# A row softmax: from tile-managed waits and two DMA queues to own semaphores, one queue in a fixed order, and loops on ScalarE

## The chip, the cores and the metric

The kernel runs on one core of a Trainium2 chip. The metric is the device time of one execution in microseconds; lower is better. A core has five engines with instruction streams of their own that meet only through semaphores: TensorE (PE, not used here), VectorE (DVE), ScalarE (ACT), GpSimd (POOL) and SyncE (SP). Beside them 16 DMA engines move data between the chip's memory and the core's on-chip memory. SP and ACT can each issue transfers, each into a DMA queue of its own; both queues are served by the same 16 DMA engines.

## The reference

```python
def setup_inputs():
    batch, seq, dim = 16, 1024, 512
    return {"x": np.random.randn(batch, seq, dim).astype(np.float32)}

def reference(x):
    x_max = np.max(x, axis=-1, keepdims=True)
    exp_x = np.exp(x - x_max)
    return (exp_x / np.sum(exp_x, axis=-1, keepdims=True)).astype(np.float32)
```

It is a softmax over 16,384 rows of 512 float32 values. All of the input, 33.55 MB, is read once and as much is written once.

## The kernel before

The rows are cut into 8 chunks of 2,048 rows. In a chunk each of the 128 partitions holds 16 rows of 512 values, 32 KB, so that a chunk is one transfer of 4,096 KB. On chip there are 6 places (`held`); chunk k lies in place k mod 6, is computed in place, and is stored from there. Chunks 6 and 7 therefore go into the places of chunks 0 and 1, once these have been stored. A chunk is handled in two groups of 8 rows a partition, so there are 16 groups, g = 0 to 15; chunk k is groups 2k and 2k + 1.

The work on one group:

- `rowmax` (line 89): DVE takes the negated maximum of each of the 8 rows in one reduction over 128 x 4,096 elements, into `shift`.
- `exps` (line 94): ACT computes exp(x + shift) row by row, 8 instructions of 128 x 512, each leaving its row's sum in `sums`. The 128 such instructions stand one after the other in ACT's program.
- `scale` (lines 105 to 114): DVE takes the reciprocal of the 8 sums. For groups 0 to 12 POOL multiplies the whole group with it in one instruction of 128 x 4,096 (line 107); for groups 13 to 15 DVE does it row by row, 8 instructions of 128 x 512 (line 114).

The order on each engine is that of the text, written out by hand: for each g the maximum of g, the exponentials of g, then the scaling of g - 1. The waits between the engines are put in by the tile layer, which owns the buffers and their semaphores.

Transfers: SP issues the loads (line 72), ACT the stores (line 75). Loads 0 to 5 are issued at the start, the very first ahead of the barrier at which all engines meet at the kernel's start (`loads_at_the_head`). Loads 6 and 7 stand in SP's program behind stores 0 and 1 and wait for them. A store stands in ACT's program between exponentials, up to two groups later than the last scaling of its chunk (`STORE_BEHIND`). Loads lie in DMA queue q1, stores in q10.

Behind the last store comes the closing work of the tile layer (line 161): SP waits for the outstanding transfers, then all engines meet twice, and the semaphores are cleared between.

Of the kernel before, what the change touches and what calls it, by code (L numbers as in the profile page):

```python
# [1 line left out]

# [4 lines left out]

F32 = mybir.dt.float32
EXP = mybir.ActivationFunctionType.Exp
AX = mybir.AxisListType.X  # L10


CHUNK = 16
CHUNKS = 8
PLACES = 6
GROUP = 8

STORE_BEHIND = [1, 1, 1, 1, 0, 0, 0, 0]

LOAD_AFTER = {0: 6, 1: 7}  # L20
ON_POOL = 13


AT_HEAD = {mybir.EngineType.SP: 1}

def loads_at_the_head(nc):

    main, body = nc.main_func.blocks[0], nc.main_func.blocks[1]  # L30
    for engine, count in AT_HEAD.items():
        loads = [
            i
            for i in body.instructions
            if i.engine == engine and type(i).__name__ == "InstDMACopy"
        ][:count]
        barrier = next(
            n
            for n, i in enumerate(main.instructions)
            if i.engine == engine and type(i).__name__ == "InstDrain"  # L40
        )
        for load in loads:
            body.instructions.remove(load)
        main.instructions[barrier:barrier] = loads


@with_exitstack
def kernel(
    ctx: ExitStack,
    tc: tile.TileContext,  # L50
    x: bass.AP,
    out: bass.AP,
):
    nc = tc.nc
    nc.at_finalize(loads_at_the_head)
    P = nc.NUM_PARTITIONS

    x_rows = x.flatten_outer_dims().rearrange("(c p r) d -> c p r d", p=P, r=CHUNK)
    out_rows = out.flatten_outer_dims().rearrange("(c p r) d -> c p r d", p=P, r=CHUNK)
    n, _, _, d = x_rows.shape  # L60
    assert n == CHUNKS

    data = ctx.enter_context(tc.tile_pool(name="data", bufs=1))
    stats = ctx.enter_context(tc.tile_pool(name="stats", bufs=6))
    held = data.tile([P, PLACES * CHUNK, d], F32, name="held")

    def place(k):
        at = (k % PLACES) * CHUNK
        return held[:, at : at + CHUNK, :]

    def load(k):
        nc.sync.dma_start(out=place(k), in_=x_rows[k])  # L72

    def store(k):
        nc.scalar.dma_start(out=out_rows[k], in_=place(k))
        if k in LOAD_AFTER:
            load(LOAD_AFTER[k])

    per = CHUNK // GROUP
    groups = CHUNKS * per  # L80
    shift, sums = [None] * groups, [None] * groups

    def rows(g):
        at = (g % per) * GROUP
        return place(g // per)[:, at : at + GROUP, :]

    def rowmax(g):
        shift[g] = stats.tile([P, GROUP], F32, name="shift", tag="shift")
        nc.vector.reduce_max(out=shift[g], in_=rows(g), axis=AX, negate=True)  # L89

    def exps(g):
        sums[g] = stats.tile([P, GROUP], F32, name="sums", tag="sums")
        for r in range(GROUP):
            nc.scalar.activation(  # L94
                out=rows(g)[:, r, :],
                in_=rows(g)[:, r, :],
                func=EXP,
                bias=shift[g][:, r : r + 1],
                scale=1.0,
                accum_out=sums[g][:, r : r + 1],  # L100
            )

    def scale(g):
        recip = stats.tile([P, GROUP], F32, name="recip", tag="recip")
        nc.vector.reciprocal(out=recip, in_=sums[g])  # L105
        if g < ON_POOL:
            nc.gpsimd.tensor_mul(  # L107
                out=rows(g),
                in0=rows(g),
                in1=recip.unsqueeze(2).to_broadcast([P, GROUP, d]),  # L110
            )
            return
        for r in range(GROUP):
            nc.vector.tensor_scalar_mul(  # L114
                out=rows(g)[:, r, :],
                in0=rows(g)[:, r, :],
                scalar1=recip[:, r : r + 1],
            )

    with tc.manual_schedule():  # L120
        for k in range(PLACES):
            load(k)
        stored = 0
        for g in range(groups):
            rowmax(g)
            exps(g)
            if g:
                scale(g - 1)
            if stored < CHUNKS and g > (stored + 1) * per - 1 + STORE_BEHIND[stored]:
                store(stored)  # L130
                stored += 1
        scale(groups - 1)
        while stored < CHUNKS:
            store(stored)
            stored += 1


# [1 line left out]
_INS = ['x']  # L139
_OUTS = [((16, 1024, 512), 'float32')]  # L140


# [23 lines left out]
```

## Time and profile before

| what | value |
|---|---|
| device time, median of 3 runs | 161.96 us (161.58 to 162.31) |
| span of the profiled execution, first to last instruction | 160.4 us |
| that execution's own device time | not listed apart from the three runs |
| DVE / ACT / POOL busy | 82.0 / 92.7 / 91.0 us |
| memory read / written | 33.55 / 33.55 MB |
| mean rate over the span | 419 GB/s |

The page of the profile gives, for one execution, the busy time of each engine; the span in 40 slices, in which a digit is the busy share in tenths; the DMA queues; the chain of work that ended last; and groups of equal instructions with their mean duration and the idle time before them. A window view gives for any stretch the busy time of each engine, the granted clock of TensorE (1.00 throughout; TensorE isn't used), the mean busy share of the 16 DMA engines, and the rate in GB/s. A packet's whole time and bytes count where it starts, so in short windows the share can exceed 1.

### The profile page before, as it was taken

What the parts mean: (1) busy time and instruction counts of PE and PEld (TensorE: products, weight loads), DVE (VectorE), ACT (ScalarE), POOL (GpSimd) and SP (SyncE); (2) the same over time, 40 slices, a digit from 0 to 9 for tenths busy, and PEclk for the clock granted to TensorE, in tenths of its full rate; (3) what the DMA queues carried; (4) which work ended last, traced back from release to release, by engine and by line L of the source; (5) the groups of instructions that cost most, each with busy time, mean ns of one, the idle gap of its engine ahead of it and who ended that gap; (6) DMA issues with size and microseconds to landing.
All of it is one profiled execution on the core that took longest, in us unless ns stands there. A gap on an engine that the chain in (4) does not pass through costs nothing.

```text
span 160.4 us, 425 instructions
## 1 busy us (share of the span) xinstructions
DVE 82.0 (51%) x56; ACT 92.7 (58%) x257; POOL 91.0 (57%) x17
## 2 busy tenths in 40 slices
DVE  0009967977977700893009920099202999671000
ACT  0003899999998996079900959409594195920000
POOL 0000039999999999999993899508995000000000
DMA  7999999999899999999999999999999999999993
GB/s 261 482 433 392 466 449 392 443 458 400 343 433 400 449 449 409 425 474 409 425 466 409 409 490 409 402 466 441 400 449 449 409 425 474 411 409 474 425 392 139
DMA packets 2307, 67.13 MB, mean 419 GB/s; under 512 B 256, under 2 KB 256, under 8 KB 256
## 3 DMA queue, kind: packets, MB, share of 16 engines
q1 hardware_dynamic: 1152, 33.55, 49.5%
q10 hardware_dynamic: 1152, 33.55, 48.5%
q14 instruction: 3, 0.02, 0.0%
HBM read 33.55 MB, written 33.55 MB: 418 GB/s over the span
## 4 chain that ended last, share of the span: by engine, by line
DMA 53%; POOL 14%; DVE 10%; ACT 7%; issue 7%; DVEq 0%; SPq 0%
DMA held<-in_x_dram 34%; DMA out_dram<-held 19%; POOL held L107 14%; ACT held L94 7%; DVE shift L89 6%; DVE held L114 4%; DVE recip L105 0%; DVEq L161 0%; SPq L72 0%; DVEq L105 0%; DVEq L89 0%
## 5 line engine op out<-in xcount | busy, mean ns | idle before, releaser
L94 ACT ACTIVATE held<-held,shift 128x512 f32<-128x512 f32 x128 | 90.6, 719 | 36.4 <-DVE shift L89 32.0
L107 POOL TENSOR_TENSOR held<-held,recip 128x4096 f32<-128x4096 f32 x13 | 90.8, 7018 | 31.5 <-DVE recip L105 31.5
L89 DVE TENSOR_REDUCE shift<-held 128x8 f32<-128x4096 f32 x16 | 70.2, 4393 | 46.9 <-DMA held<-in_x_dram 46.9
L94 ACT ACTIVATION_READ_ACCUMULATOR held<-held,shift 128x1 f32 x128 | 25.3, 198 | 0.0
L105 DVE RECIPROCAL recip<-sums 128x8 f32<-128x8 f32 x16 | 3.2, 200 | 16.0 <-ACT held L94 16.0
L114 DVE TENSOR_SCALAR held<-held,recip 128x512 f32<-128x512 f32 x24 | 9.8, 483 | 0.1
L94 ACT ACT_TABLE_LOAD x1 | 1.3, 1283 | 12.3 <-DMA held<-in_x_dram 12.3
L150 POOL MEMSET const-float32-0.0<- 128x1 f32 x1 | 0.1, 99 | 0.2 <-issue 0.2
L150 POOL MEMSET const-bfloat16-1.0<- 128x1 bf16 x1 | 0.1, 102 | 0.0
L150 POOL MEMSET const-uint8-127<- 128x1 uint8 x1 | 0.1, 102 | 0.0
L150 POOL MEMSET const-float32-1.0<- 128x1 f32 x1 | 0.1, 99 | 0.0
## 6 DMA issues: line engine op xcount, KB each, us to landing
held<-in_x_dram SPq DMA_DIRECT2D x8, 4096.0 KB, 41.8
out_dram<-held ACTq DMA_DIRECT2D x8, 4096.0 KB, 28.0
```

What stands on the lines that cost most here:

```text
L89: nc.vector.reduce_max(out=shift[g], in_=rows(g), axis=AX, negate=True)
L94: nc.scalar.activation(out=rows(g)[:, r, :], in_=rows(g)[:, r, :], func=EXP, bias=shift[g][:, r : r + 1], scale=1.0, accum_out=sums[g][:, ...
L105: nc.vector.reciprocal(out=recip, in_=sums[g])
L107: nc.gpsimd.tensor_mul(out=rows(g), in0=rows(g), in1=recip.unsqueeze(2).to_broadcast([P, GROUP, d]),)
L114: nc.vector.tensor_scalar_mul(out=rows(g)[:, r, :], in0=rows(g)[:, r, :], scalar1=recip[:, r : r + 1],)
L150: nc = _bacc.Bacc("TRN2", target_bir_lowering=False, num_devices=1)
```

## The change

The kernel is written anew around the same chunks, places and groups, with these differences:

- The three statistics lie in memory of their own, one column for each group (128 columns each), and the buffers are allocated outside the tile layer.
- The tile layer is closed (`tc.close()`) right behind the issue of the six first loads. What it does at its end, the two meetings of all engines, then stands there in the program. Everything behind it waits on semaphores of the kernel's own: one for each load (`loaded`), each store (`stored`) and each chunk's scaling (`scaled`), and one each for maxima, exponentials and reciprocals. `take` waits until a semaphore has n and takes n off again.
- All transfers are issued by SP into one queue, in the order of `ORDER`: loads 0 to 5, stores 0 to 2, loads 6 and 7, stores 3 to 7. Ahead of each store SP waits for both groups of its chunk, ahead of loads 6 and 7 for stores 0 and 1. At the end SP waits for stores 2 to 7.
- ACT's exponentials become two loops at run time: 12 turns over groups 0 to 11 and 4 turns over groups 12 to 15, each turn with a wait, eight exponentials whose addresses come from registers, and a jump back. The table for exp is loaded ahead of the first wait.
- POOL scales groups 0 to 11 and DVE groups 12 to 15, both with one instruction of 128 x 4,096 a group (line 144 of the new kernel).
- DVE's order stays: the maximum of g, then the reciprocal and, from group 12, the product of g - 1.

```diff
-STORE_BEHIND = [1, 1, 1, 1, 0, 0, 0, 0]
-LOAD_AFTER = {0: 6, 1: 7}
-ON_POOL = 13
+ORDER = [("L", k) for k in range(PLACES)] + [
+    ("S", 0), ("S", 1), ("S", 2), ("L", 6), ("L", 7),
+    ("S", 3), ("S", 4), ("S", 5), ("S", 6), ("S", 7),
+]
+ON_VECTOR = (12, 13, 14, 15)
...
-    def load(k):
-        nc.sync.dma_start(out=place(k), in_=x_rows[k])
-
-    def store(k):
-        nc.scalar.dma_start(out=out_rows[k], in_=place(k))
-        if k in LOAD_AFTER:
-            load(LOAD_AFTER[k])
...
+    def take(engine, semaphore, n):
+        engine.wait_ge(semaphore, n).then_inc(semaphore, -n)
...
+    with tc.manual_schedule():
+        for _, k in ORDER[:PLACES]:
+            first = nc.sync.dma_start(out=place(k), in_=x_rows[k])
+            first.then_inc(loaded[k], 16)
+            tc.no_tile_sem_insts.add(first.ins.name)
+    tc.close()
+    tc.compile()
+
+    reused = set()
+    for what, k in ORDER[PLACES:]:
+        if what == "L":
+            if k >= PLACES:
+                take(nc.sync, stored[k - PLACES], 16)
+                reused.add(k - PLACES)
+            nc.sync.dma_start(out=place(k), in_=x_rows[k]).then_inc(loaded[k], 16)
+        else:
+            take(nc.sync, scaled[k], PER)
+            nc.sync.dma_start(out=out_rows[k], in_=place(k)).then_inc(stored[k], 16)
...
     def scale(g):
-        recip = stats.tile([P, GROUP], F32, name="recip", tag="recip")
-        nc.vector.reciprocal(out=recip, in_=sums[g])
-        if g < ON_POOL:
-            nc.gpsimd.tensor_mul(...)
-            return
-        for r in range(GROUP):
-            nc.vector.tensor_scalar_mul(...)
+        engine, ready = (
+            (nc.vector, to_vector) if g in ON_VECTOR else (nc.gpsimd, to_pool)
+        )
+        take(nc.vector, expd, 1)
+        nc.vector.reciprocal(out=stats(recip, g), in_=stats(sums, g)).then_inc(ready, 1)
+        take(engine, ready, 1)
+        engine.tensor_mul(
+            out=rows(g),
+            in0=rows(g),
+            in1=stats(recip, g).unsqueeze(2).to_broadcast([P, GROUP, d]),
+        ).then_inc(scaled[g // PER], 1)
...
+    nc.scalar.preload_act_table(EXP)
+
+    def exps(first, turns):
+        with nc.scalar.Fori(0, turns) as i:
+            take(nc.scalar, maxed, 1)
+            for r in range(GROUP):
+                row = held[:, bass.ds(i * GROUP + r, 1), :]
+                at = bass.ds(i * GROUP + (first * GROUP + r), 1)
+                act = nc.scalar.activation(
+                    out=row, in_=row, func=EXP,
+                    bias=shift[:, at], scale=1.0, accum_out=sums[:, at],
+                )
+            act.then_inc(expd, 1)
+
+    exps(0, RING)
+    exps(RING, GROUPS - RING)
+
+    for k in range(CHUNKS):
+        if k not in reused:
+            take(nc.sync, stored[k], 16)
```

More of the change, by code (lines that the diff above doesn't have):

```diff
@@ L61 @@
     assert n == CHUNKS
-    data = ctx.enter_context(tc.tile_pool(name="data", bufs=1))
-    stats = ctx.enter_context(tc.tile_pool(name="stats", bufs=6))
-    held = data.tile([P, PLACES * CHUNK, d], F32, name="held")
+    held = nc.alloc_sbuf_tensor("held", [P, PLACES * CHUNK, d], F32).ap()
+    shift = nc.alloc_sbuf_tensor("shift", [P, GROUPS * GROUP], F32).ap()
+    sums = nc.alloc_sbuf_tensor("sums", [P, GROUPS * GROUP], F32).ap()
+    recip = nc.alloc_sbuf_tensor("recip", [P, GROUPS * GROUP], F32).ap()
+    loaded = [nc.alloc_semaphore(f"loaded{k}") for k in range(CHUNKS)]
+    stored = [nc.alloc_semaphore(f"stored{k}") for k in range(CHUNKS)]
+    maxed = nc.alloc_semaphore("maxed")
+    expd = nc.alloc_semaphore("expd")
+    to_pool = nc.alloc_semaphore("to_pool")
+    to_vector = nc.alloc_semaphore("to_vector")
+    scaled = [nc.alloc_semaphore(f"scaled{k}") for k in range(CHUNKS)]
+    def take(engine, semaphore, n):
+        engine.wait_ge(semaphore, n).then_inc(semaphore, -n)
     def place(k):
@@ L69, in place @@
         return held[:, at : at + CHUNK, :]
-    def load(k):
-        nc.sync.dma_start(out=place(k), in_=x_rows[k])
-    def store(k):
-        nc.scalar.dma_start(out=out_rows[k], in_=place(k))
-        if k in LOAD_AFTER:
-            load(LOAD_AFTER[k])
-    per = CHUNK // GROUP
-    groups = CHUNKS * per
-    shift, sums = [None] * groups, [None] * groups
-    def rows(g):
-        at = (g % per) * GROUP
-        return place(g // per)[:, at : at + GROUP, :]
-    def rowmax(g):
-        shift[g] = stats.tile([P, GROUP], F32, name="shift", tag="shift")
-        nc.vector.reduce_max(out=shift[g], in_=rows(g), axis=AX, negate=True)
@@ L91, in exps @@
-    def exps(g):
-        sums[g] = stats.tile([P, GROUP], F32, name="sums", tag="sums")
-        for r in range(GROUP):
[L94 to L101, printed above, removed]
-    def scale(g):
-        recip = stats.tile([P, GROUP], F32, name="recip", tag="recip")
-        nc.vector.reciprocal(out=recip, in_=sums[g])
-        if g < ON_POOL:
[L107 to L111, printed above, removed]
-            return
[L113 to L135, printed above, removed]
+    def rows(g):
+        at = (g % RING) * GROUP
+        return held[:, at : at + GROUP, :]
@@ new lines, in stats @@
+    def stats(t, g):
+        return t[:, g * GROUP : (g + 1) * GROUP]
+    with tc.manual_schedule():
[15 more added lines that the diff above has]
+            nc.sync.dma_start(out=out_rows[k], in_=place(k)).then_inc(stored[k], 16)
@@ new lines, in rowmax @@
+    def rowmax(g):
+        if g % PER == 0:
+            take(nc.vector, loaded[g // PER], 16)
+        nc.vector.reduce_max(
+            out=stats(shift, g), in_=rows(g), axis=AX, negate=True
+        ).then_inc(maxed, 1)
+    def scale(g):
+        engine, ready = (
[9 more added lines that the diff above has]
+        ).then_inc(scaled[g // PER], 1)
@@ new lines @@
+    for g in range(GROUPS):
+        rowmax(g)
+        if g:
+            scale(g - 1)
+    scale(GROUPS - 1)
+    nc.scalar.preload_act_table(EXP)
[6 more added lines that the diff above has]
+                act = nc.scalar.activation(
+                    out=row,
+                    in_=row,
+                    func=EXP,
+                    bias=shift[:, at],
+                    scale=1.0,
+                    accum_out=sums[:, at],
+                )
+            act.then_inc(expd, 1)
```

13 lines of the change are left out of this document (added).

## The prediction

> **What bounds the kernel now.** I read the page from the top: busy shares, the 40 slices, the DMA queues, then the chain of waits, and last windows of the span.
>
> ```profile
> span 160.4 us, 425 instructions
> DVE 82.0 (51%) x56; ACT 92.7 (58%) x257; POOL 91.0 (57%) x17
> DMA  7999999999899999999999999999999999999993
> q1 hardware_dynamic: 1152, 33.55, 49.5%
> q10 hardware_dynamic: 1152, 33.55, 48.5%
> q14 instruction: 3, 0.02, 0.0%
> held<-in_x_dram SPq DMA_DIRECT2D x8, 4096.0 KB, 41.8
> ```
>
> No compute engine is busy for 60% of the span. The DMA line reads 9 nearly everywhere, and the two data queues (q1 loads, q10 stores) together hold 98.0% of the 16 DMA engines' span. So the sixteen transfers of 4096 KB (4.194 MB) set the time, and the question for any edit is whether it changes how fast the DMA engines run, when they start, or what follows them. Next, the rate in windows:
>
> ```profile
> core 0: us, DVE busy (x) ACT busy (x) POOL busy (x), PEclk, DMA share, GB/s
> 3.00:37.00 34.00, 20.89 (x8) 21.56 (x58) 14.20 (x3) 1.00 1.01 435
> 37.00:42.00 5.00, 3.84 (x3) 5.00 (x15) 5.00 (x1) 1.00 1.02 347
> 42.00:123.00 81.00, 38.33 (x18) 54.63 (x154) 71.60 (x11) 1.00 1.00 433
> 123.00:157.00 34.00, 18.95 (x29) 11.53 (x32) 0.00 (x0) 1.00 1.00 431
> ```
>
> The last column is what moved. Loads alone in one queue (3 to 37) run at 435 GB/s, loads and stores mixed from two queues (42 to 123) at 433, stores alone in one queue (123 to 157) at 431. One stretch stands out: at the first store (37 to 42) only 347 GB/s. What is missing there is (435 - 347) x 5 / 435 = 1.0 us of the DMA engines' time. Then the head and the tail, from the chain, the stores' landings, the wait list of SP's queue and two short windows:
>
> ```profile
> 0.00 12.25 DMA held<-in_x_dram
> ```
> ```profile
> L75 ACTq DMA_DIRECT2D out_dram<-held x8: 338/338/377, 36.8 to 145.0; - x8
> DMA to landing us min/median/max: 14.5/28.0/41.5
> ```
> ```profile
> SPq L161 <- PEq L161: 0.6, 2, 0.4
> ```
> ```profile
> 157.60:158.00 0.40, 0.00 (x0) 0.00 (x0) 0.00 (x0) 1.00 0.01 0
> 158.00:158.40 0.40, 0.00 (x0) 0.00 (x0) 0.00 (x0) 1.00 0.20 82
> ```
>
> The first load has landed whole at 12.25. The last store is issued at 145.0; it has the queue almost to itself, so the minimum of 14.5 us is its own, and it lands at 159.5. From there to 160.4 stands 0.9 us of closing work, 0.6 us of it SP waiting twice for the other engines. In 157.6 to 158.0 no packet starts, then exactly one does (82 GB/s x 0.4 us = 33 KB, a 32 KB row): one DMA engine is behind the rest.
>
> **A sum that closes on the present.** At 433 GB/s a transfer takes 4.194 / 0.433 = 9.69 us. First landing 12.25, fifteen more: 12.25 + 15 x 9.69 = 157.6. The last landing is at 159.5, so 1.9 us are left to explain. The dent at the first store is 1.0. For the rest I look at q14, instruction fetches, three in the span; one of them, the queue line of the window 31 to 32:
>
> ```profile
> q14 instruction: 1, 0.01, 1.9%
> ```
>
> 1.9% of 16 engines' 1 us is 0.30 us on one DMA engine. Three of them are 0.9, if they fall on the engine that ends last, which is my reading of that lone packet and not shown. 157.6 + 1.0 + 0.9 = 159.5, as observed; + 0.9 = 160.4. The profiled execution's own time is not listed apart; I put 1.6 us around its span, median 161.96 less 160.4, so the sum is made level with the median (the runs spread from 161.58 to 162.31).
>
> **The change, part by part.** (1) All transfers go through SP's queue in a fixed order, each store behind a wait for its own chunk. The DMA engines keep their rate by the 435 and 431 rows, since one queue alone already fills them, provided the next transfer is always issued before the one ahead ends. The clock for this check comes from these rows:
>
> ```profile
> 16.73 0.72 ACT L94 ACTIVATE held<-held,shift 128x512 f32<-128x512 f32 x1 [3.12 <-DVE shift L89]
> ...
> 22.39 0.71 ACT L94 ACTIVATE held<-held,shift 128x512 f32<-128x512 f32 x1
> ...
> 22.80 62.82 POOL L107 TENSOR_TENSOR held<-held,recip 128x4096 f32<-128x4096 f32 x9 [22.37 <-DVE recip L105]
> ```
> ```profile
> L107 POOL TENSOR_TENSOR held<-held,recip 128x4096 f32<-128x4096 f32 x13 | 90.8, 7018 | 31.5 <-DVE recip L105 31.5
> L89 DVE TENSOR_REDUCE shift<-held 128x8 f32<-128x4096 f32 x16 | 70.2, 4393 | 46.9 <-DMA held<-in_x_dram 46.9
> L105 DVE RECIPROCAL recip<-sums 128x8 f32<-128x8 f32 x16 | 3.2, 200 | 16.0 <-ACT held L94 16.0
> L114 DVE TENSOR_SCALAR held<-held,recip 128x512 f32<-128x512 f32 x24 | 9.8, 483 | 0.1
> ```
>
> Eight exponentials take 22.39 - 16.73 = 5.66 us, POOL 7.02 a group from 22.8, DVE 4.4 a maximum. Steps of 9.69 from 12.25 end the loads L1 to L5 at 21.9, 31.6, 41.3, 51.0, 60.7, then S0, S1, S2 at 70.4, 80.1, 89.8, L6 and L7 at 99.5 and 109.2, S3 to S7 at 118.9, 128.6, 138.3, 147.9, 157.6. POOL has chunks 0 to 4 ready at 36.8, 50.9, 64.9, 79.0, 93.0; they are wanted at 60.7, 70.4, 80.1, 109.2, 118.9. L6 waits for S0's landing (70.4) and is wanted at 89.8; L7 for S1's (80.1), wanted at 99.5. Behind L7's wait on SP stand S3 and all later stores, and who waits for them is only the DMA queue: S3 is issued at 80.5 instead of 79.0, 28 us early. Group 11's reciprocal stands behind the maximum of group 12 on DVE, which waits for L6: 99.5 + 4.4 = 103.9, then POOL to 111.1; S5 is wanted at 128.6. The last two chunks are scaled on DVE. Group 12: maximum to 103.9, exponentials to 109.6, reciprocal 0.2 and product 4.4 to 114.2; maximum 14 to 118.6, group 13's product to 123.2, so S6 has 15 us. Maximum 15 to 127.6, product 14 to 132.2, exponentials 15 to 133.3, product 15 to 137.9; S7 is wanted at 147.9. Ten us of slack is the least. Step (1): 0.
>
> The product of 4,096 elements on DVE isn't in the trace. The reduction over as many takes 4.4, POOL's two-input product 7.02, the eight small ones now used 8 x 0.48 = 3.9 at most. I take 4.4, the same engine and element count. At 7.02 S7 would be ready 4 x 2.6 = 10.4 later, at 148.3, 0.4 behind: that is the loss bound; a gain has nothing to reach.
>
> [...]
>
> (3) The dent at the first store. The new kernel too has a first store, behind L5, but in a ring already in use. The trace can't say whether the store or the fresh queue q10 costs the 1.0: bounds 0 and 1.0 stay (a gain of 1.0 or none). No later start of a transfer shows a dent in the 433 window. I take half, a gain of 0.5.
>
> (4) ScalarE's 128 unrolled exponentials (257 busy instructions on ACT) become two loop bodies of eight, DVE's 24 small products become four. Less program means fewer fetches: between three as now and none, so a gain of 0 to 0.9. I take one left, a gain of 0.6: ACT's program is by far the longest and it shrinks most. The register steps and the branch of each turn aren't in the trace; their nearest rows are one exponential, 0.7 us a turn above and nothing below (the queue ahead of the engine), so 16 groups would end 11 us later at worst if they counted from the start, but the last four groups, after L6, only 2.8: inside the ten us.
>
> (5) The two all-engine meetings behind the last landing move ahead of the first wait, right behind the loads' issue, where the first load's 12.25 us hide them. With that cover gone they would cost 0.6 again. At the end only SP's wait for the landing stays, 0.1. Gain 0.8; bounds 0 (if what surrounds the kernel takes it back) and 0.9. The issue of eight stores leaves ACT (0.34 each) for SP, which has nothing else to do; the table load ahead of the first wait and the statistics in their own memory are hidden in the same 12.25.
>
> Sum: 160.4 - 0.5 - 0.6 - 0.8 = 158.5, + 1.6 = 160.1. The other way round: 157.6 + 0.5 + 0.3 + 0.1 + 1.6 = 160.1. With both open terms gone whole 159.3; with neither 161.2. I forecast **160.1**.
>
> **Rivals.** (A) Each turn between loads and stores inside one queue costs what the first store costs now. There are three turns (L5 to S0, S2 to L6, L7 to S3): 157.6 + 3.0 + 0.3 + 0.1 + 1.6 = 162.6. For it: the dent is real. Against: from 42 to 123 loads and stores alternate at 433 without a trace of it. 8%.
>
> (B) Slower: the loops fetch their code anew at every turn. ACT jumps back 11 + 3 = 14 times; if each jump brings a fetch of 0.30 us onto the DMA engine that ends last, landing is 157.6 + 0.5 + 14 x 0.3 = 162.3, + 0.1 + 1.6 = 164.0. It decides from 7 such fetches (157.6 + 0.5 + 2.1 + 1.7 = 161.9), and is slower by 0.5% from 10. For it: fetches do ride on the same DMA engines. Against: straight code of 257 instructions brought only three, so a body of eight exponentials is far smaller than one fetch. [...] 11%.
>
> (C) The change doesn't do what it says: the fetches stay three because they belong to other engines, the first store dents as now, and the closing 0.8 comes back in part outside the span. Then between 161.2 and 162.0, say 161.6. For it: nothing shows whose the fetches are. 9%.
>
> **How the numbers follow.** A measurement of this kernel tells 0.5%, so faster means below 161.15 and slower above 162.77. The forecast, 159.3 to 161.1, has 72% and is all faster; A and C, 17%, lie within; B is slower, 11%. The range is 158.9 to 162.2: it takes in C and the forecast with the 0.4 by which runs of before stray below their median, and leaves out A and B.
>
> **What would show it.** Right: q10 gone, DMA slices at 9 up to the last two, no wait of SP's for a chunk's scaling that outlasts the transfer ahead, last landing near 158.4 and the span ending 0.1 behind it, q14 at one or none. Step 3 is read in the windows around the first store (about 58 to 66): 435 throughout or a dent to about 390 or 350. A: dents at 61, 90 and 109. B: q14 above ten, and a lone DMA engine ending several us late. Wrong altogether if a slice inside the span drops below 9 because a store was issued late; then S7, with ten us, is the first suspect.

## The result and the profile after

The changed kernel takes 160.19 us at the median of 4 runs (160.09 to 160.32); beside it the kernel before took 161.77 (161.52 to 162.31). The ratio is 0.9886, 95% interval 0.9853 to 0.992: about 1.1% faster. The forecast was 160.1. Times are medians of fast runs; one slower run, of e8 below (162.78), is left out. On the chip of e5 below the kernel before took 162.03 (16 runs) and the changed one 160.18, so the gain lies between 1.6 and 1.9 us.

The page of the changed kernel, the lines that answer to those of before:

```profile
span 159.0 us, 740 instructions
DVE 90.6 (57%) x36; ACT 92.0 (58%) x257; POOL 84.0 (53%) x16
DMA  7999999999999999999999999999999999999995
q1 hardware_dynamic: 2304, 67.11, 98.8%
q14 instruction: 2, 0.02, 0.0%
DVE held L144 3%
```

The DMA line again reads 9 from the second slice to the last but one, now from one queue (q10 is gone), 98.8% in place of 49.5 + 48.5. The instruction fetches are two, not three. The chain that ended last is of no use here: the page follows semaphores, and those that `take` sets back itself it doesn't link to their setter; it gives only the last product on DVE. So I go by windows (the last column is GB/s):

```profile
3.00:57.00 54.00, 35.94 (x15) 41.08 (x114) 33.44 (x5) 1.00 1.00 433
57.00:62.00 5.00, 4.52 (x2) 5.00 (x15) 5.00 (x2) 1.00 0.98 354
62.00:123.00 61.00, 34.03 (x15) 36.19 (x103) 45.34 (x7) 1.00 1.00 433
123.00:157.00 34.00, 16.11 (x6) 9.75 (x28) 0.00 (x0) 1.00 1.01 434
...
```

The rates are those of before, the dent at the first store included: it has only moved from 37 to 57 us, to where that store now stands. What closes the kernel, from the stores' line and SP's waits:

```profile
L127 SPq DMA_DIRECT2D out_dram<-held x8: 332/338/851, 37.7 to 141.0; - x8
DMA to landing us min/median/max: 17.9/28.3/38.6
```
```profile
SPq L94 <- SPq L94: 150.3, 11, 33.6
SPq L116 <- PEq L116: 0.4, 2, 0.3
```

The last store is issued at 141.0 and lands 17.9 us later, at 159.0, where the span ends. The meetings (L116) now stand at the start. The third thing to read is which DMA engine ends last. The traces of both kernels have 16 landing times for every transfer (those of the changed kernel's last store run from 157.77 to 158.96); I take them as one for each of the 16 DMA engines. The median of the last store's 16 and the last of them, in us of the span, for the two kernels (how far the last is behind the median is called its lag below):

```
          median of 16   last of 16   last behind median   span
before       158.26        159.58            1.32          160.41
changed      158.16        158.96            0.80          158.99
```

The typical DMA engine gained 0.10 us from the whole redesign. The last one gained 0.52 more, and 0.83 - 0.03 = 0.80 came from behind the landing: 1.42 of span in all. With what lies around the span (1.79 and 1.33, see e2) the two executions are 1.9 apart; by this estimate (160.41 + 1.79 = 162.2) the one of before was longer than the median.

Where the lag arose can be read from the landings of the earlier transfers. In the kernel before it was 0.29 at L1 and 1.04 at L2, with a fetch at 31.2 us between them; it was 1.21 at S0, 1.17 at S3 and 1.41 at S4. The fetch at 100.6 may have to do with that second rise (the loads that ran beside the stores went from 2.42 behind at L5 to 3.10 at L6); the one at 138.3 left it as it was (1.34 at S5). In the changed kernel it goes from 0.15 at S2 to 0.45 at L6 and 0.59 at L7, without a fetch, then slowly to 0.80 at S7; no step of more than 0.11 stands at its two fetches (110.4 and 132.3 us).

### The profile page after: what moved, and what is told of

Its sections match the earlier page's. It is cut to its first block, busy times and chain, and to the rows that moved or that the text cites. A ratio compares the mean times of both kernels' runs of the same rounds, so it can differ in the third digit from the quotient of the medians.

```text
span 159.0 us, 740 instructions
## 1 busy us (share of the span) xinstructions
DVE 90.6 (57%) x36; ACT 92.0 (58%) x257; POOL 84.0 (53%) x16
## 3 DMA queue, kind: packets, MB, share of 16 engines
q1 hardware_dynamic: 2304, 67.11, 98.8%
## 5 line engine op out<-in xcount | busy, mean ns | idle before, releaser
L165 ACT ACTIVATE held<-held,shift x128 | 90.3, 706 | 40.0 <-ACTq L94 40.0
L144 POOL TENSOR_TENSOR held<-held,recip 128x4096 f32<-128x4096 f32 x12 | 83.8, 7018 | 28.1 <-POOLq L94 28.1
L165 ACT ACTIVATION_READ_ACCUMULATOR held<-held,shift x128 | 23.8, 186 | 0.0
L144 DVE TENSOR_TENSOR held<-held,recip 128x4096 f32<-128x4096 f32 x4 | 18.3, 4576 | 0.6
```

The source lines that it names most:

```text
L144: engine.tensor_mul(out=rows(g), in0=rows(g), in1=stats(recip, g).unsqueeze(2).to_broadcast([P, GROUP, d]),).then_inc(scaled[g // PER], 1)
L165: act = nc.scalar.activation(out=row, in_=row, func=EXP, bias=shift[:, at], scale=1.0, accum_out=sums[:, at],)
```

## The experiments

Twelve experiments ran, in groups on one chip each. The table has what the experiments are read by; the landing times and the span are of one profiled execution, the time is the median of the runs, "around" is time less span at the median (each run lists both).

```
                                  time    runs from - to    around   landing of the last store   fetches
                                                                     median of 16 / last behind
e1  unrolled                     161.34   160.60 - 161.95    1.33        158.13 / 1.11              3
e2  two meetings at the end      161.28   161.14 - 161.45    1.78        158.06 / 0.73              2
e3  small early store            160.29   160.08 - 160.43    1.30        158.18 / 0.70              2
e4  unrolled, two queues         160.61   160.17 - 161.20    1.32        158.22 / 0.79              3
e5  as changed                   160.18   160.12 - 160.37    1.33        158.01 / 0.81              2
e6  less program                 160.30   160.10 - 161.38    1.30        157.91 / 2.11              1
e7  two queues, loops            160.12   160.01 - 160.27    1.33        158.22 / 0.69              2
e8  seven turns                  160.62   160.28 - 162.28    1.31        158.54 / 0.37              2
e9  idle code on TensorE         162.20   161.73 - 162.55    1.43        158.09 / 2.61              3
e10 POOL scales all              160.25   160.12 - 160.33    1.33        158.11 / 0.81              2
e11 unrolled again               161.02   160.43 - 161.86    1.33        158.02 / 1.63              3
e12 idle code, two queues        161.89   161.29 - 162.40    1.43        158.15 / 2.33              3
```

**e2, the closing work put back.**

```diff
     for k in range(CHUNKS):
         if k not in reused:
             take(nc.sync, stored[k], 16)
+    for _ in range(2):
+        nc.all_engine_barrier()
```

> The changed kernel with two meetings of all engines added behind the last wait. If the closing work was worth 0.8 us because it stood behind the last landing, the time is 161.0 (0.8 above the changed kernel's 160.2) and the span ends 0.8 behind the landing. Rival: what surrounds the kernel waits for all engines in any case and takes the 0.8 in; then 160.2 to 160.4.

Measured 161.28, 1.1 above the changed kernel's 160.2 and 0.3 above the forecast, with runs that spread over 0.3. SP's wait list shows the meetings twice, at the start (L116) and at the end (L184):

```profile
SPq L94 <- SPq L94: 150.3, 11, 33.7
SPq L184 <- PEq L184: 0.5, 2, 0.3
SPq L116 <- PEq L116: 0.4, 2, 0.3
```

The span ends 159.46 - 158.79 = 0.67 behind the landing, a little less than the theory's 0.8 (these two meetings have no clearing of semaphores between them, as the kernel before has). But the time around the span also grew, from 1.32 to 1.78, and 1.79 is what the runs of the kernel before show. So the meetings cost more than the span tells: 0.64 inside (0.67 less the 0.03 of the changed kernel) and 0.46 outside. The rival expected the surroundings to take the cost in; they added to it.

**e1 and e11, ScalarE unrolled.**

```diff
-    exps(0, RING)
-    exps(RING, GROUPS - RING)
+    for g in range(GROUPS):
+        exps(g)        # the same eight exponentials, with fixed addresses
```

> The changed kernel with ScalarE's 128 exponentials unrolled, as before, in place of the two loops. If the instruction fetches on the DMA engines are largely ScalarE's, q14 goes from 2 to 3 or more in the span and the time rises by 0.3 us for each that falls on the DMA engine that ends last: 160.4 to 160.8. Rival: the fetches belong to the other engines, or fall on a DMA engine that isn't last; then the time stays at 160.2 within 0.1.

> The unrolled kernel a second time, for a second trace and more runs: the first gave 160.6 to 161.95, and its trace was of the shortest. Theory: 161.2 to 161.4 at the median, three fetches, of which ScalarE's two fall on one DMA engine and put it 1.1 us or more behind the median. Rival: the first series was a whim of that chip; then 160.2 to 160.5.

161.34 and, on another chip, 161.02: 0.8 to 1.1 above the looped kernel (above e1's forecast, a little below e11's), and the runs spread over 1.4 us where the looped kernel's spread over 0.3. Both traces have three fetches. The page's queue lines of e1:

```profile
q1 hardware_dynamic: 2304, 67.11, 98.6%
q14 instruction: 3, 0.02, 0.0%
```

They come at 36.9, 77.1 and 132.1 us. At the first two ScalarE stands at the same places of its program in e1, e4 and e11 (67 and 188 to 198 recorded instructions), at the third VectorE does (65), and a fetch near 131 with VectorE at 65 is also in the looped kernels. So by their places ScalarE's straight code brings two and its loops one; no trace names the engine that a fetch is for. In e11 the lag goes from 0.39 to 0.51 across the first of them (L2 to L3), from 0.44 at S0's landing at 71 to 1.01 at S1's at 81 across the second, and from 1.03 at L6's at 100 to 1.64 at L7's at 110, where no fetch is near. So the two fetches go with 0.1 and 0.6 (0.3 each was expected), and as much again came without one.

**e9 and e12, fetches without work.** To have the price of a fetch apart from ScalarE, TensorE, otherwise idle, was given straight code:

```diff
+    nc.vector.memset(blank, 0.0).then_inc(gate, 1)
+    for _ in range(400):
+        nc.tensor.wait_ge(gate, 1)
+    take(nc.tensor, gate, 1)
```

> The changed kernel with 400 waits that are already satisfied in the program of TensorE, which does nothing else; they run off early, among the first loads. It adds about three instruction fetches and no other work on the DMA engines. Theory, a fetch costs the DMA engine that it falls on 0.3 us itself and 0.3 in the packet behind it, for good: with three on one engine that engine is 1.8 us behind, and the time is 161.4 to 162.0; with them on different engines 160.4 to 160.8. Rival: a fetch by itself is taken in by the queue; 160.2 within 0.15.

162.20, 2.0 above; 1.8 of it is the lag (2.61 against 0.81 in e5 and e10), 0.1 lies around the span. The added fetch was one, not three, and larger (16 KB and 1.0 us, where each of the three of before moved 8 KB in 0.31). The queue lines of the window 29 to 31 of e9:

```profile
q1 hardware_dynamic: 36, 0.85, 100.4%
q8 instruction: 1, 0.02, 3.1%
```

3.1% of 16 engines' 2 us is 1.0 us on one DMA engine. The last engine's lag goes from 0.29 at the landing of L1 to 1.63 at L2, and stays there until the turn to the stores at 59 us, where one packet takes 3.07 us (the next longest there 2.11, elsewhere 1.21) and the lag becomes 2.71. It isn't made up: at the last store's landing it is 2.61. In the tail of e9 a lone packet shows it (one row of 32 KB is 33 GB/s over 1 us):

```profile
157.00:158.00 1.00, 0.00 (x0) 0.00 (x0) 0.00 (x0) 1.00 0.16 66
158.00:159.00 1.00, 0.00 (x0) 0.00 (x0) 0.00 (x0) 1.00 0.00 0
159.00:160.00 1.00, 0.00 (x0) 0.00 (x0) 0.00 (x0) 1.00 0.08 33
```

Every other packet has begun by 158; the last begins behind 159. That one engine stayed behind from the fetch to the end of the span is as the theory had it; its price was too low (1.63 - 0.29 = 1.34 of lag with one fetch, against 0.6), and the second loss was not in it. That fetch, long packet and last landing are of one engine is inferred from the lag, since the trace doesn't name a packet's engine. Whether a late engine pays once more at a sharp turn was then asked of the two-queue kernel of e7 below, with the same code on TensorE:

> The kernel with two queues and loops (loads 1 to 5 in ScalarE's queue, 160.12 us) with the same 400 satisfied waits on TensorE. In one queue they cost 2.0 us: in its trace 1.3 us came on one DMA engine with the fetch at 30 us, and another 1.1 on the last engine at the turn to the stores at 59 us. Theory: an engine that is behind pays once more at a sharp turn, and mixed queues have no such turn at that time; so two queues keep only the fetch's own price, 161.3 to 161.6. Rival: a late engine costs the same in either arrangement; 162.0 to 162.3.

161.89, between the two. Its trace shows the fetch (the last engine goes from 0.41 to 1.53 behind) and the second loss, which did not go away: it came at 108 us, at the turn from L7 to S3, with a packet of 2.15 us. So in both traces a second loss stands at a turn; the forecast that two queues would spare it failed. Why a late engine loses more at a turn is open.

**e6, fewer fetches still.** ScalarE's turns of four exponentials, VectorE's maxima and reciprocals of chunks 3 to 5 taken whole:

```diff
-        with nc.scalar.Fori(0, turns) as i:
+        with nc.scalar.Fori(0, 2 * turns) as i:
...
+    rowmax(6, 2)
+    scale(5)
+    rowmax(8, 2)
+    scale(6, 2)
+    rowmax(10, 2)
```

> The changed kernel with less program: ScalarE's loops have four exponentials a turn in place of eight (24 and 8 turns), and VectorE takes the maxima of chunks 3 to 5 and the reciprocals of chunks 3 to 5 whole instead of in two halves, nine instructions fewer. Theory: the two fetches left are ScalarE's and VectorE's, at fixed places of their programs; both vanish, and the DMA engine that ends last is behind the median by 0.4 us, as at the start, in place of 0.8: 159.8 us, with no wider spread of the runs. Rival: the lag of the last DMA engine isn't made by fetches; then 160.2 within 0.1, fetches or none.

Of the two fetches one is left, at 145 us, when only SP still has work. The time did not follow: 160.30, the rival's number, with four of seven runs within 160.10 to 160.30, like the changed kernel's. The profiled run was the longest of them (161.38), and tells more than a good one:

```profile
q14 instruction: 1, 0.01, 0.0%
```

Its last engine is 0.22 behind at the landing of S2, 1.13 at L6 and 1.67 at L7, with no fetch near; one packet at 91.3 us took 1.99. So an engine fell behind without a fetch too, here at the turn from S2 to L6. Lag rose beside fetches (e9) and away from them (e6), and the late fetches (110 and 132 us) cost the changed kernel nothing that I could measure.

**e3, a store early.** 64 KB of zeros into rows that store 0 writes again:

```diff
+    nc.vector.memset(blank, 0.0).then_inc(blanked, 1)
+    take(nc.scalar, blanked, 1)
+    nc.scalar.dma_start(out=out_rows[0][:, 0, 0:128], in_=blank).then_inc(touched, 16)
```

> The changed kernel with one store of 64 KB zeros (128 partitions x 512 bytes, into rows that store 0 writes again later) issued by ScalarE right at the start, in its own queue. If the dent of about 0.9 us is the price of the first write to the output, wherever it stands, it is paid during the first loads, the windows 57 to 62 read 433 GB/s, and the time is 159.4 if paying it early is free, or 160.2 if it costs the same there. Rival, the dent is the turn from loads to stores inside a queue: the window 57 to 62 still reads about 354 GB/s and the time is 160.2 to 160.4.

160.29, and the dent stays. The windows of e3:

```profile
57.00:62.00 5.00, 4.56 (x2) 5.00 (x15) 5.00 (x2) 1.00 0.96 367
62.00:123.00 61.00, 34.12 (x15) 36.43 (x103) 45.49 (x7) 1.00 1.01 434
```

The 64 KB written early didn't pay for it (367 GB/s in the window of the dent, against the 354 of the changed kernel).

**e4 and e7, two queues.** In e4 the unrolled kernel's stores are issued from ScalarE, at the places of before; in e7 the looped kernel's loads 1 to 5 go into ScalarE's queue.

```diff
+    for g in range(GROUPS):                            # e4
+        exps(g)
+        if done < CHUNKS and g > (done + 1) * PER - 1 + STORE_BEHIND[done]:
+            take(nc.scalar, scaled[done], PER)
+            nc.scalar.dma_start(out=out_rows[done], in_=place(done)).then_inc(stored[done], 16)
+            done += 1
...
-            first = nc.sync.dma_start(out=place(k), in_=x_rows[k])
+            queue = nc.scalar if k else nc.sync        # e7
+            first = queue.dma_start(out=place(k), in_=x_rows[k])
```

> The changed kernel with ScalarE unrolled and the eight stores issued from ScalarE's queue, at the places among the exponentials where they stood before; own semaphores, early closing and DVE's products stay. My theory: the number of queues and the order are worth nothing as long as a transfer is always waiting, so it is within 0.2 us of the unrolled kernel with one queue. Rival: mixing loads and stores from two queues is what cost the old kernel its time; then it is 0.5 us or more above the unrolled one.

> The changed kernel, loops and all, with loads 1 to 5 issued into ScalarE's queue; load 0, loads 6 and 7 and the stores stay in SP's, so that loads and stores mix from 38 us to about 80. Theory: the number of queues is worth nothing; 160.2 within 0.15. Rival, from the unrolled pair, where two queues were 0.7 us below one: two queues are better in themselves; then 159.5.

e5, the changed kernel without an edit, ran beside e6, e7 and e8 to compare them with:

> The changed kernel once more, on the chip of the next three, to compare them with: 160.2 us within 0.2, two instruction fetches in the span, one of ScalarE's and one of VectorE's.

It took 160.18, with the two fetches. With loops the number of queues is worth nothing: 160.12 against 160.18, and no version beat the changed kernel by more than that. Unrolled, two queues are 0.73 below one (160.61 against 161.34); neither e4's theory (within 0.2) nor its rival (0.5 or more above) had that, and why is open. In the traces of e1 and e4 the median engine lands at 158.1 and 158.2; what differs is the lag, 1.11 against 0.79. So the loops are worth 0.8 to 1.1 in one queue, but with two queues only 160.61 - 160.12 = 0.5 (e4 and e7 don't put the same transfers into the second queue). The kernel before took 161.97 on e4's chip (22 runs): 1.4 of the gain is there with the straight code and two queues kept.

And the dent: in e4 it is where the first store stands again, and not at 57:

```profile
37.00:42.00 5.00, 3.92 (x3) 5.00 (x15) 5.00 (x2) 1.00 0.98 367
57.00:62.00 5.00, 0.48 (x2) 5.00 (x15) 5.00 (x2) 1.00 1.02 439
```

So it goes with the first full store, in the queue of the loads or in a fresh one. The packets of the changed kernel show more: 18 of them that start between 57.4 and 59.2 us take 1.9 on average in place of 1.21, about 0.8 us more per DMA engine. And the median landing of L5 is 10.5 us after L4's, where the loads before and S0 behind it take 9.7. So the time is lost on the last load, before it lands, and not behind it.

**e8, seven turns.**

```diff
-ORDER = [("L", k) for k in range(PLACES)] + [
-    ("S", 0), ("S", 1), ("S", 2), ("L", 6), ("L", 7),
+ORDER = [("L", k) for k in range(PLACES - 1)] + [
+    ("S", 0), ("L", 5), ("S", 1), ("L", 6), ("S", 2), ("L", 7),
     ("S", 3), ("S", 4), ("S", 5), ("S", 6), ("S", 7),
 ]
```

> The changed kernel with its one queue in the order five loads, S0, L5, S1, L6, S2, L7, S3 to S7: seven turns between loads and stores in place of three, nothing wanted before it is ready. Theory: only the first store dents the rate, and later turns are free; 160.2 within 0.15. Rival A of the prediction: each turn from loads to stores costs what the first does, 0.7 to 0.9 us; two more of these turns, 161.6 to 162.0.

160.62: 0.44 more for four more turns, so neither. The windows:

```profile
47.00:52.00 5.00, 3.92 (x3) 5.00 (x15) 5.00 (x2) 1.00 0.89 321
52.00:57.00 5.00, 3.85 (x2) 5.00 (x15) 5.00 (x1) 1.00 1.02 439
57.00:62.00 5.00, 4.47 (x2) 5.00 (x15) 5.00 (x2) 1.00 1.02 439
```

One deep dent at the first store, none like it at the turns behind it (62 to 123 reads 431). The best run, 160.28, is close to the changed kernel's; the others scatter upwards. A later turn has a small price, 0.11 at the median. The trace is of that best run; in it the median engine lands at 158.54, 0.53 later than in e5, and the last one only 0.37 behind it. Where the longer runs lose isn't shown.

**e10, slower scaling at the end.**

```diff
-ON_VECTOR = (12, 13, 14, 15)
+ON_VECTOR = ()
```

> The changed kernel with POOL scaling groups 12 to 15 as well (7.02 us each in place of 4.4 on VectorE). By the prediction's clock the last chunk is then ready about 141 to 146 instead of 141, still ahead of the 148 at which the queue wants it: 160.2 within 0.15, nothing on the path. Rival: the compute of the last chunks sets the end after all; then 161 to 165.

160.25: the scaling of the last chunks is not on the path, as the prediction's clock said. POOL takes its 7.01 a group, and SP's last issue is at 140.3, not later than 141.0: by the order of its program VectorE, rid of the products (4.42 to 5.03 each), can take its maxima earlier.

```profile
L144 POOL TENSOR_TENSOR held<-held,recip 128x4096 f32<-128x4096 f32 x16 | 111.7, 7014 | 28.1 <-POOLq L94 28.1
L127 SPq DMA_DIRECT2D out_dram<-held x8: 332/338/944, 37.5 to 140.3; - x8
```

## Why the prediction was right, and where it was not

The forecast of 160.1 met 160.19. What bounds the kernel and two of the three gains came out as predicted; that the number met so closely is partly luck, since two errors offset each other: the span was forecast 0.5 too short, the time around it 0.3 too long.

- **The bound and step (1), the queue never runs dry: right.** 433, 433 and 434 GB/s outside the dent. The clock held within a few us: S0, S2, S5 and S6 were issued at 37.7, 65.6, 112.4 and 125.7 (expected 36.8, 64.9, 111.1, 123.2), S7 at 141.0 against 137.9. Lost on the way were, among others, the 1.0 by which L6 landed late and 0.6 on VectorE's first product. Seven us of slack were left where ten were expected, and e10 shows that they are slack.

```profile
111.58 5.03 DVE L144 TENSOR_TENSOR held<-held,recip 128x4096 f32<-128x4096 f32 x1
...
136.50 4.42 DVE L144 TENSOR_TENSOR held<-held,recip 128x4096 f32<-128x4096 f32 x1
```

  The product that the trace of before didn't have takes 4.42, as taken, and 5.03 once, when POOL was at work beside it for the first 0.75 us; that this is why wasn't tried.
- **One queue or two.** By the rates (433 GB/s with both kinds in two queues before, 433 and 434 in the one queue of the changed kernel) and by e7 against e5 (0.06 us) it changes nothing here. In the unrolled pair two queues are 0.73 better, but in the two traces the median DMA engine lands at the same time, and only the engine that ends last differs.
- **Step (3), half of the dent: wrong.** "I take half, a gain of 0.5." The gain was 0: the dent came back whole, 354 GB/s against 347, in a queue already in use. It came with the first full store (367 GB/s at 37 us in e4, 321 at 47 us in e8), and a small early store didn't take it away (367 at 57 us in e3). The median engine's landing gained 0.10, all changes taken together. No run was without the dent, so what it costs at the end isn't shown; in the changed kernel L5 lands 0.8 late by it.
- **Step (4), the fetches: near in size, in part by luck, and only in part by its mechanism.** Expected was a gain of 0.6 from two fetches fewer, 0.30 us each. One fetch went, and the lag fell by 0.52 in the two profiles. The fetches are not alike: in the kernel before the lag rose by 0.75 at the early one (31.2 us), by about 0.2 around the second and not at the third. That is near the 0.9 of three times 0.30 in all, but the whole lag there was 1.32. The two that the changed kernel keeps are late and cost it nothing measurable, yet it has a lag of 0.80, and e6 shows 2.11 with one late fetch. The loops are worth 0.5 (two queues) to 1.1 (one). e9 has the clearest price of an early fetch, of 16 KB there: 1.3 us where it falls and 1.1 more at the next turn. What makes the rest of the lag is open. The jumps and register steps cost nothing that shows: eight exponentials take 5.65 us from turn to turn in the loops, 5.65 to 5.66 before.
- **Step (5), the closing work: right inside the span, undersized as a whole.** 0.80 of span against 0.8 forecast. The sum then added "1.6 us around its span" to both kernels; measured, it is 1.8 before and 1.3 after. The two meetings are worth 1.1 (e2), the largest part of the gain.
- **The sum.** The span was forecast at 158.5 and is 159.0: of the difference 0.4 is step 3's (a median landing 0.10 earlier in place of 0.5), 0.1 step 4's. What lies around was put at 1.6 and is 1.3 in the profiled run of 160.32. Of the signs named ahead, q10 is gone, the slices stay at 9 and the span ends right behind the last landing; but q14 is at two, not at one or none, and that landing is at 158.96, not near 158.4.
- **Rivals.** (A) at 1.0 a turn is refuted by e8's 0.11 a turn at the median. (B) is refuted: fourteen jumps back, and two fetches in all. (C) had one part right, the dent; one of the three fetches went, and outside the span the early closing saved another 0.5 in place of being taken back.

## What to carry to other kernels

With the DMA engines full from end to end here (98.0% of their span in two queues, 98.8% in one), the number of queues hardly moved the typical DMA engine (its last landing is at 157.9 to 158.3 in every kernel here but e8's); look at the one that ends last and at what stands behind its landing. Work that all engines do together at the end cost more here than its part of the span (1.1 us against 0.64, e2): move it to where the first load hides it (in the changed kernel the meetings are over at 4.0 us, and the first load lands at 12.34). Straight code on TensorE, otherwise idle, came with a fetch of 16 KB that took 1.0 us of one DMA engine's time, and the lag that rose there to 1.63 us at 32 of 160 us was still there at the end, at 2.61 (e9).

## What the runs showed of the hardware that I had not expected

- The time around the span is not a constant: 1.79 us where the engines meet behind the last landing (the kernel before and e2), 1.32 where they met early, 1.43 where TensorE had 400 waits besides (e9, e12). Why wasn't tried.
- One 16 KB fetch for an idle engine, at 30 us of a kernel of 160, went with 2.0 us more (e9), at the fetch and at the first turn behind it.
- A DMA engine that was behind lost more at a turn between loads and stores (a packet of 3.07 us in e9, where the next longest took 2.11, and one of 2.15 in e12, where the others took about 1.2), and one fell behind there with no fetch at all (a packet of 1.99 in e6). What decides which engine and when is open.
